# A decoder layer on one core: order of the experts' gate and up products, start of the expert sums, and spread of LN2's vectors changed

## The chip, the cores and the metric

One Trainium2 chip, of which the kernel uses one core: TensorE (PE), VectorE (DVE), ScalarE (ACT), GpSimd (POOL), SyncE (SP, which here only issues DMAs) and 16 DMA engines. The metric is device time of one execution in microseconds, lower is better: the median of several runs. One execution is profiled apart.

## The reference

One layer on 512 tokens of width 1024. A token mixer (dilated attention, sliding-window attention with sinks, gates, output projection) is followed by LN1, then a mixture of 32 experts of which each token takes 4, then LN2:

```
x   = layer_norm(alpha * x + mix, ln1_g, ln1_b)          # alpha = 2 ** 0.25, eps = 1e-5
top_val, top_idx = top_k(x @ router_w + router_b, 4); gates = softmax(top_val)
gt  = min(xb @ w_gate[e] + b_gate[e], 7);  up = clip(xb @ w_up[e] + b_up[e], -7, 7)
ys  = (gt * sigmoid(1.702 * gt) * (up + 1)) @ w_down[e] + b_down[e]
ffn = sum over a token's 4 experts of gate * ys
out = layer_norm(alpha * x + ffn, ln2_g, ln2_b)
```

All weights are float32, and all 32 experts' weights (32 x 12 MB) are read.

## The kernel before

**Up to the experts.** The mixer is a long sequence of TensorE matmuls over chunks of `w_in`, `w_proj` and `w_out`. At its start `first_chunk` loads x and the first `w_in` chunk in quarters on SP's queue, while POOL's queue writes zeros from the tile `warm` into `acc_dram`, the DRAM tensor of the expert sums, in 16 pieces. `norm_tile(t)` does LN1 for one of four token tiles; the result y stays in `r_tiles[t]` and is written to `y_dram` by POOL's queue (for t = 0 also to 128 spare rows). The router follows: `route_places` finds each token's place with its experts, `slots` turns places into row indices and gathers an expert's rows of y with an indirect DMA on POOL's queue, `rank_experts` orders the experts by their number of tokens, `route_weights` makes the softmax weights.

**The experts.** Experts run in an order by rank (`TURNS`). The 18 with most tokens have two blocks of rows: block A of 64 rows (its products are 128 x 512 in PSUM) and block B of 32 rows (128 x 256). The other 14 have block A alone; experts 0 and 1 of the order have two blocks, 2 and 3 one, the last three one. `ffn` does one expert: its 12 weight chunks (4 gate, 4 up, 4 down, each 1.05 MB and two rows of K) go through `load_expert` to a ring of 21 slots in several pools, of which the slots of `ring_d` lie where `r_tiles` were. `load_expert` is called in the order of use, and the loads stand on SP's queue in that order, each behind the last reader of its slot; eight DMAs of SP are under way at most. `gate_up(n)` does bias, gate and up products of block n (0 is A, 1 is B); `glu(n)` the clamps, gelu and product on VectorE and ACT; then `transposed` (TensorE, copied by ACT) and `down`. Gate and up of block A have a PSUM bank each (tags `a0`, `a1`), those of B share one (tag `b`). `add_rows` adds the weighted rows to `acc_dram` with an indirect DMA on POOL's queue. `midway` computes the index lists of the expert after the next.

Each engine's instructions run in the order in which the program's scheduler puts them, which is that of the text unless an instruction isn't ready by its estimate; `tc.issue_after(ins)` keeps what it encloses behind `ins` on the same engine.

**The end.** The rows of the last expert are not added in DRAM: `goes` is a 0/1 matrix with which TensorE spreads `ys_last` over the tokens into `psf`. Before that, `free_tiles(6)` takes six ring slots: LN2's two vectors come in as broadcasts to 128 partitions, y as four loads (`y_last`), the sums as four loads (`r_last`), and `load_sums` makes alpha * y + sum on VectorE. A loop under `tc.If` handles experts with more rows than their blocks hold; with these inputs its body doesn't run, but all engines pass its test (line 981; line 980 loads the number into registers). `last_rows(t)` does `psf`, the sum with its mean, and the variance; `last_norm(t)` normalizes on ACT, multiplies by g on VectorE, adds b on POOL or VectorE, and stores 512 KB.

Of the kernel before, what the change touches and what calls it, by code (L numbers as in the profile page):

```python
# [8 lines left out]
F32 = mybir.dt.float32  # L9
# [48 lines left out]
def decoder_kernel(tc, d):  # L58
# [19 lines left out]
    def load_chunk(src, n, name, pool=None):  # L78
        t = (pool or ring_a).tile([P, 2048], F32, name=name, tag="w")
        nc.sync.dma_start(t[:, :n], src[:, :n])  # L80
        return t

    n_loaded = [0]

# [8 lines left out]
    def load_expert(src, name):  # L93

        ring = next_ring()
        if ring is not None:
            t = load_chunk(src, 2048, name, ring)
            return [t[:, :1024], t[:, 1024:]]
        t = [spl.tile([P, 1024], F32, name=f"{name}{n}", tag=f"w{n}") for n in "hl"]
        for n in range(2):  # L100
            nc.sync.dma_start(t[n], src[:, n * 1024:(n + 1) * 1024])
        return t
# [32 lines left out]
    for n in range(8):  # L135
        mm(ps, warm[:, :P], warm, True, True)

    dpool = tc.alloc_tile_pool(name="dp", bufs=1, space=DRAM)
    y_dram = dpool.tile([S + P, D], F32, name="y_dram")
    acc_dram = dpool.tile([S + P, D], F32, name="acc_dram")  # L140
# [377 lines left out]
    ring_c = tc.alloc_tile_pool(name="ring_c", bufs=RING[3], side="right")  # L518
    rings.append(ring_c)
    mo1 = tc.alloc_tile_pool(name="mo1", bufs=1, side="right")  # L520
    p_y = tc.alloc_tile_pool(name="p_y", bufs=1, side="right")
# [28 lines left out]

    last = {}

    def norm_stats(r, sums, sq, pool, name):
# [5 lines left out]
        A.activation(rs, rs, AF.Sqrt, bias=C[:, C_COL + 4:C_COL + 5], scale=1.0 / D)  # L559
        V.reciprocal(rs, rs)  # L560
        return nmu, rs
# [16 lines left out]
    def norm_tile(t):  # L578
# [4 lines left out]
        with tc.high_priority():  # L583
            for n in range(2):
                cs = slice(n * 512, (n + 1) * 512)
                V.scalar_tensor_tensor(y[:, cs], y[:, cs], ALPHA, mix[t][n], op0=ALU.mult, op1=ALU.add,
                                       accum_out=sums[:, n:n + 1])
            sq = yT[0].rearrange("p k c -> p (k c)").bitcast(BF16)
            nmu, rs = norm_stats(y, sums, sq, p_ln, f"a{t}")
        for n in range(2):  # L590
# [218 lines left out]
    def ffn(e, chunk, state, sw, xt, midway=None, next_rows=None):  # L809
# [10 lines left out]

        def gate_up(n):
            slots_n, pieces, tiles = (64, 2, 4) if n == 0 else (32, 4, 2)
            for g in range(2):
                packed_mm(n, pg[n][g], sel[:, :slots_n], bh[:, g * D:(g + 1) * D], n == 0 or g == 0, False)
            for g in range(2):
                for k in range(KT):
                    packed_mm(n, pg[n][g], xt[n][:, k % tiles, k // tiles, :], chunks[4 * g + k // 2][k % 2],
                              False, k == KT - 1)

        def glu(n):  # L830
            gt, up = pg[n]
            w = 512 if n == 0 else 256
            h = mo.tile([P, w], F32, name=f"up{n}{e}", tag=f"up{n}")
            V.tensor_scalar(gt, gt, 7.0, None, op0=ALU.min)  # L834
            A.activation(gt, gt, AF.Gelu_apprx_sigmoid)  # L835
            V.tensor_scalar(h, up, 7.0, -7.0, op0=ALU.min, op1=ALU.max)  # L836
            V.scalar_tensor_tensor(h, h, 1.0, gt, op0=ALU.add, op1=ALU.mult)
            return h
# [44 lines left out]
    def rank_experts():  # L883
# [12 lines left out]
        V.tensor_copy(order_i, order[0:1])  # L896

    rank_experts()
    for tp in range(2):
# [3 lines left out]
    rings.append(tc.alloc_tile_pool(name="ring_d", bufs=RING[4], side="right", reuse_waits="tile"))  # L903

    def expert(i):
        def midway():
            if i == 0:
                for e in range(FIXED):
                    sws[e] = late_weights(e, states[e], first_info[e], psX, "t")
            if i + 2 < NE:  # L910
                r = TURNS[i + 2]
# [24 lines left out]
    ys_last, = expert(NE - 1)  # L936
    free = free_tiles(6)
    goes = free[0][:, :S]
# [7 lines left out]
    ln2 = free[1].rearrange("p (n c) -> p n c", n=2)  # L946
    nc.sync.dma_start(ln2[:, 0, :], d["ln2_g"].partition_broadcast(P))
    nc.sync.dma_start(ln2[:, 1, :], d["ln2_b"].partition_broadcast(P))
    tiles = [t.rearrange("p (n c) -> p n c", n=2) for t in free[2:]]
    y_last = [tiles[t // 2][:, t % 2, :] for t in range(NT)]  # L950
    r_last = [tiles[2 + t // 2][:, t % 2, :] for t in range(NT)]
# [56 lines left out]


    def last_rows(t):  # L1010

        r = r_last[t]
        part_sums = mo.tile([P, 2], F32, name=f"fsums{t}", tag="fsums", bufs=NT)
        for n in range(2):
            cs = slice(n * 512, (n + 1) * 512)
            ps = psG.tile([P, S], F32, name=f"psf{t}{n}", tag=f"a{n}")
            half = slice(64 * n, 64 * n + 64)
            ts = slice(t * P, (t + 1) * P)
            mm(ps, goes[half, ts], ys_last[half, :], True, True, (64 * n, 0))
            V.scalar_tensor_tensor(r[:, cs], ps, 1.0, r[:, cs], op0=ALU.mult, op1=ALU.add,  # L1020
                                   accum_out=part_sums[:, n:n + 1])
        sq = mo.tile([P, 512], F32, name=f"fsq{t}", tag="up0").bitcast(BF16)
        nmu, rs = norm_stats(r, part_sums, sq, mo, f"f{t}")
        V.tensor_tensor(nmu, nmu, rs, op=ALU.mult)  # L1024
        return nmu, rs
# [23 lines left out]
def _consts():  # L1049
# [8 lines left out]
    c[:, C_COL + 3] = i % 32  # L1058
    c[:, C_COL + 4] = EPS
    for n, m in enumerate((64, 32)):  # L1060
        pieces = P // m
# [73 lines left out]
```

## Time and profile before

| | us |
|---|---|
| median of 3 runs | 1568.25 |
| lowest, highest | 1567.65, 1575.2 |
| the profiled execution | 1572.44 |
| its span, first to last instruction | 1570.6 |

Of the span TensorE is busy 94%, VectorE 30%, ACT 21%, POOL 10%; the mean granted TensorE clock is 0.973 of full speed. DMA moves 477.38 MB. A span of a matmul is modelled, so a busy TensorE is not TensorE at its peak. Times in all rows are microseconds from the span's start.

### The profile page before, as it was taken

How to read it: one execution, taken by the hardware profiler on the slowest of the kernel's cores; microseconds unless marked ns; L12 is line 12 of the kernel's file. 1: busy time of each engine (PE TensorE's matmuls, PEld its weight loads, DVE VectorE, ACT ScalarE, POOL GpSimd, SP SyncE). 2: the span in 40 equal slices, each digit the busy share in tenths (PEclk: the TensorE clock that was granted, in tenths of full speed). 3: DMA queues.
4: the chain of work that ended last, by engine and by line, in shares of the span. 5: the costliest groups of instructions: out<-in, count | busy, mean ns of one | idle time of the engine just before them, and what ended most of it. 6: DMA issues, size and time to landing. Idle time of an engine off the chain costs nothing. (4 is left out here: it accounts for less than half of the span.)

```text
span 1570.6 us, 24882 instructions
## 1 busy us (share of the span) xinstructions
PE 1469.7 (94%) x10022; PEld 808.3 (51%) x10022; DVE 467.0 (30%) x1348; ACT 322.3 (21%) x697; POOL 161.7 (10%) x133
## 2 busy tenths in 40 slices
PE   8999999999996999999999899989999899889872
PEld 6987777788885444535344353325335253323220
DVE  3133667764337412111211121111211112111105
ACT  4233556633323101100101011000100001000003
POOL 2000000000001011111201111111211111111002
PEclk9989999999997999999999999999999999999995
DMA  8111110332387599999999999999999999999992
GB/s 311 59 50 54 54 44 18 137 133 90 131 344 299 220 362 410 408 404 409 405 405 408 408 408 407 405 409 407 409 411 400 412 400 407 412 393 412 410 404 89
DMA packets 85527, 477.38 MB, mean 304 GB/s; under 512 B 10528, under 2 KB 13088, under 8 KB 39968
## 3 DMA queue, kind: packets, MB, share of 16 engines
q1 hardware_dynamic: 73440, 449.78, 70.7%
q0 software_dynamic: 11968, 25.96, 6.3%
q8 instruction: 81, 1.33, 0.3%
q14 instruction: 38, 0.31, 0.1%
HBM read 458.40 MB, written 17.30 MB: 303 GB/s over the span
## 5 line engine op out<-in xcount | busy, mean ns | idle before, releaser
L834 DVE TENSOR_SCALAR pga<-pga 128x512 f32<-128x512 f32 x32 | 22.4, 699 | 385.1 <-PE pga L806 374.4
L798 POOL DMA_INDIRECT acc_dram<-ys,ix x49 | 78.1, 1594 | 365.7 <-issue 131.9
L734 POOL DMA_INDIRECT xg<-y_dram,ix x50 | 61.0, 1220 | 501.4 <-issue 358.6
L836 DVE TENSOR_SCALAR up<-pga 128x512 f32<-128x512 f32 x32 | 22.1, 691 | 230.7 <-PE pga L806 230.7
L790 ACT COPY th<-pth 128x512 f32<-128x512 f32 (+1 forms) x50 | 25.3, 506 | 293.8 <-PE pm L64 257.6
L117 DVE TENSOR_TENSOR wlin<-win,whin 128x1024 fp32r<-128x1024 f32 x42 | 51.2, 1224 | 115.3 <-ACT whin L116 109.9
L849 ACT ACTIVATE ys<-pda,sw 128x512 f32<-128x512 f32 x32 | 22.0, 688 | 229.2 <-PE pda L806 229.2
L835 ACT ACTIVATE pga<-pga 128x512 f32<-128x512 f32 x32 | 18.6, 582 | 245.5 <-DVE pga L834 245.5
L116 ACT CAST whin<-win 128x1024 fp32r<-128x1024 f32 x42 | 44.1, 1050 | 65.8 <-PE psk L64 15.3
L64 PE MATMUL psg<-xh,wlin 128*128 128x512 f32 x128 | 50.1, 392 | 0.0
L64 PE MATMUL psg<-xh,whin 128*128 128x512 f32 x128 | 50.1, 391 | 0.0
L64 PE MATMUL psg<-xl,whin 128*128 128x512 f32 x128 | 49.9, 390 | 0.0
L790 ACT COPY tx<-ptx 128x512 f32<-128x512 f32 (+1 forms) x50 | 24.4, 516 | 100.6 <-PE ptx L788 100.6
L806 PE MATMUL pga<-we_l,tx 128*64 128x512 f32 x152 | 42.3, 597 | 2.5 <-DMA we_l<-in_w_exp_dram 2.5
L806 PE MATMUL pga<-we_h,tx 128*64 128x512 f32 x152 | 42.4, 597 | 1.7 <-DMA we_h<-in_w_exp_dram 1.7
L540 POOL MEMSET obf<- 128x128 bf16 x1 | 0.2, 205 | 412.5 <-DVE merged L512 412.5
L834 DVE TENSOR_SCALAR pgb<-pgb 128x256 f32<-128x256 f32 x18 | 7.8, 432 | 104.2 <-PE pgb L806 104.2
L64 PE MATMUL mx<-whwo,merged 128*128 128x512 f32 x128 | 38.1, 400 | 0.0
L739 DVE TENSOR_SCALAR sel<-C,order 96x64 bf16<-96x64 f32 x30 | 7.4, 247 | 92.3 <-PE pdb L806 92.3
L64 PE MATMUL psv<-wlin,xh 128*128 128x256 f32 x96 | 34.4, 358 | 0.0
L64 PE MATMUL psv<-whin,xl 128*128 128x256 f32 x96 | 34.4, 358 | 0.0
L64 PE MATMUL psv<-whin,xh 128*128 128x256 f32 x96 | 34.4, 358 | 0.0
(1310 smaller groups left out, 3018.4 us busy)
## 6 DMA issues: line engine op xcount, KB each, us to landing
we_h<-in_w_exp_dram SPq DMA_DIRECT2D x54, 512.0 KB
we_l<-in_w_exp_dram SPq DMA_DIRECT2D x54, 512.0 KB
win<-in_w_in_dram SPq DMA_DIRECT2D x21, 1024.0 KB
wpj<-in_w_proj_dram SPq DMA_DIRECT2D x8, 640.0 KB
wo<-in_w_out_dram SPq DMA_DIRECT2D x4, 1024.0 KB
y_dram<-r POOLq DMA_DIRECT2D x5, 512.0 KB, 3.4
x<-in_xT_dram SPq DMA_DIRECT2D x4, 512.0 KB
acc_dram<-warm POOLq DMA_DIRECT2D x16, 128.0 KB, 6.3
```

What stands on the lines that cost most here:

```text
L64: T.matmul(out, lhsT, rhs, start=start, stop=stop)
L116: A.copy(wh[:, :n], src)
L117: V.tensor_tensor(wl[:, :n], src, wh[:, :n], op=ALU.subtract)
L734: G.indirect_dma_start(out=x, out_offset=None, in_=table, in_offset=bass.IndirectOffsetOnAxis(ap=ix[:, 0:1], axis=0))
L739: V.tensor_scalar(sel, C[:96, C_COL + 3:C_COL + 4].to_broadcast([96, 64]), which, None, op0=ALU.is_equal)
L790: A.copy(t, pt.rearrange("p (b h s) -> p b h s", b=tiles, h=pieces))
L798: G.indirect_dma_start(out=acc, out_offset=bass.IndirectOffsetOnAxis(ap=state[0][n][1][:, 0:1], axis=0), in_=ys[n], in_offset=None, comput ...
L806: last["mm"] = T.matmul(out[m * h:m * h + m, :], lhsT, rhs[:, h * w:(h + 1) * w], start=start, stop=stop, tile_position=(0, m * h), skip_g ...
L834: V.tensor_scalar(gt, gt, 7.0, None, op0=ALU.min)
L835: A.activation(gt, gt, AF.Gelu_apprx_sigmoid)
L836: V.tensor_scalar(h, up, 7.0, -7.0, op0=ALU.min, op1=ALU.max)
L849: A.mul(y, pd[n], sw()[n])
```

## The change

1. The zero writes to `acc_dram` go. After LN1 of a token tile, POOL's queue writes y to `acc_dram` too: tiles 0 to 2 behind their write to `y_dram`, tile 3 ahead of `rank_experts`. The tail no longer loads y and no longer adds alpha * y. To make up for alpha, the softmax denominators are multiplied by alpha, and LN2's epsilon is divided by alpha squared.
2. `gate_up` and `glu` are split. The order of an expert's products becomes: biases A, gate A, biases B, gate B, up A, up B; clamp and gelu of gate A stand behind gate A, those of gate B behind up B.
3. `ln2_rows`, in `midway` of the last expert: LN2's vectors are loaded as rows of one partition, spread by four matmuls with a row of ones, and copied from PSUM by ACT.
4. The tail: the sums' loads stand behind the last weight load on SP's queue; `psf` uses eight PSUM banks in place of two; two tiles are under way at a time in place of three; all adds of b on VectorE; the last tile is normalized on VectorE with two fused operations per half; each tile is stored in two halves.

```diff
-    for t in range(NT):
-        for n in range(4):
-            G.dma_start(acc_dram[t * P:(t + 1) * P, n * 256:(n + 1) * 256], warm.bitcast(F32))
...
         G.dma_start(y_dram[t * P:(t + 1) * P, :], y)
         if t == 0:
             G.dma_start(y_dram[S:, :], y)
+        if t < NT - 1:
+            G.dma_start(acc_dram[t * P:(t + 1) * P, :], y)
...
+        V.tensor_scalar(se, se, ALPHA, None, op0=ALU.mult)
         V.reciprocal(se, se)
...
-        gate_up(0)
-        hA = glu(0)
+        biases(0)
+        products(0, 0)
+        gate_of(0)
         if n_blocks > 1:
             with tc.issue_after(last["mm"].ins):
-                gate_up(1)
-            hB = glu(1)
+                biases(1)
+                products(1, 0)
+        with tc.issue_after(last["mm"].ins):
+            products(0, 1)
+        hA = gated(0)
+        if n_blocks > 1:
+            with tc.issue_after(last["mm"].ins):
+                products(1, 1)
+            gate_of(1)
+            hB = gated(1)
...
+    G.dma_start(acc_dram[(NT - 1) * P:S, :], r_tiles[NT - 1])
     rank_experts()
...
+    def ln2_rows():
+
+        row, out = free_tiles(2)
+        ones = mo.tile([1, P], F32, name="ones")
+        G.memset(ones, 1.0)
+        nc.sync.dma_start(row[:1, :D], d["ln2_g"][None, :])
+        nc.sync.dma_start(row[:1, D:], d["ln2_b"][None, :])
+        for n in range(4):
+            cs = slice(n * 512, (n + 1) * 512)
+            ps = (psG, psD)[n % 2].tile([P, S], F32, name=f"psl{n}", tag="b")
+            mm(ps, ones, row[:1, cs], True, True)
+            A.copy(out[:, cs], ps)
+        ln2.extend((out[:, :D], out[:, D:]))
...
-    free = free_tiles(6)
+    free = free_tiles(3)
...
-    nc.sync.dma_start(ln2[:, 0, :], d["ln2_g"].partition_broadcast(P))
-    nc.sync.dma_start(ln2[:, 1, :], d["ln2_b"].partition_broadcast(P))
...
-    for t in range(NT):
-        nc.sync.dma_start(y_last[t], y_dram[t * P:(t + 1) * P, :])
...
             nc.sync.dma_start(r_last[t], acc_dram[t * P:(t + 1) * P, :])
-            V.scalar_tensor_tensor(r_last[t], y_last[t], ALPHA, r_last[t], op0=ALU.mult, op1=ALU.add)
-
-    load_sums()
+
+    with tc.issue_after(last["load"].ins):
+        load_sums()
...
+    banks = [(psG, "a0"), (psG, "a1"), (psG, "b"), (psD, "b"), (psX, "t"), (psX, "t"), (psX, "t"), (psD, "a")]
...
     def last_norm(t, nmu, rs):
         r = r_last[t]
-        A.activation(r, r, AF.Identity, bias=nmu, scale=rs)
+        g, b = ln2
+        if t < NT - 1:
+            V.tensor_tensor(nmu, nmu, rs, op=ALU.mult)
+            A.activation(r, r, AF.Identity, bias=nmu, scale=rs)
         for n in range(2):
             cs = slice(n * 512, (n + 1) * 512)
-            V.tensor_tensor(r[:, cs], r[:, cs], ln2[:, 0, cs], op=ALU.mult)
-            (V if n and t > 1 else G).tensor_tensor(r[:, cs], r[:, cs], ln2[:, 1, cs], op=ALU.add)
-        nc.sync.dma_start(d["out"][t * P:(t + 1) * P, :], r)
+            if t < NT - 1:
+                V.tensor_tensor(r[:, cs], r[:, cs], g[:, cs], op=ALU.mult)
+                V.tensor_tensor(r[:, cs], r[:, cs], b[:, cs], op=ALU.add)
+            else:
+                V.scalar_tensor_tensor(r[:, cs], r[:, cs], nmu, g[:, cs], op0=ALU.add, op1=ALU.mult)
+                V.scalar_tensor_tensor(r[:, cs], r[:, cs], rs, b[:, cs], op0=ALU.mult, op1=ALU.add)
+            nc.sync.dma_start(d["out"][t * P:(t + 1) * P, cs], r[:, cs])
...
-    stats = [last_rows(t) for t in range(3)]
+    stats = [last_rows(t) for t in range(2)]
     for t in range(NT):
+        if t + 2 < NT:
+            stats.append(last_rows(t + 2))
         last_norm(t, *stats[t])
-        if t + 3 < NT:
-            stats.append(last_rows(t + 3))
```

`biases(n)` and `products(n, g)` hold the loops of `gate_up` for one block and one of gate (g = 0) and up (g = 1); `gate_of(n)` clamps and activates the gate, `gated(n)` clamps up and multiplies.

## Rows read from the trace of the kernel before

**Rows 1.** Busy time by stage: stretch, length, engines (instructions), clock, DMA share, GB/s.
```profile
17.00:485.00 468.00, 467.40 (x2427) 381.24 (x2427) 230.71 (x503) 193.45 (x455) 2.97 (x5) 0.98 0.31 113
485.00:511.00 26.00, 13.90 (x90) 11.32 (x88) 18.92 (x57) 7.52 (x15) 5.53 (x6) 0.59 0.94 351
...
800.00:1500.00 700.00, 657.74 (x5158) 271.68 (x5150) 117.23 (x446) 68.69 (x138) 94.08 (x67) 1.00 1.02 407
```
**Rows 2.** The same view in steps of 5 us, where the weight stream starts.
```profile
515.00:520.00 5.00, 5.00 (x26) 1.55 (x24) 0.71 (x4) 0.00 (x0) 0.00 (x0) 1.00 0.00 0
...
560.00:565.00 5.00, 5.00 (x74) 2.22 (x74) 1.38 (x2) 0.00 (x0) 0.00 (x0) 1.00 0.56 145
```
**Rows 3.** Timeline of SP's queue, 440 to 620: start, length, DMA issued.
```profile
527.46 0.34 SPq L80 DMA_DIRECT2D we__4536<-in_w_exp_dram  x1
...
545.60 0.33 SPq L80 DMA_DIRECT2D we__4634<-in_w_exp_dram  x1
...
563.28 0.33 SPq L80 DMA_DIRECT2D we__4750<-in_w_exp_dram  x1
...
571.45 0.33 SPq L101 DMA_DIRECT2D we_l<-in_w_exp_dram  x1
...
580.08 0.33 SPq L80 DMA_DIRECT2D we__4803<-in_w_exp_dram  x1
...
591.90 0.33 SPq L80 DMA_DIRECT2D we__4948<-in_w_exp_dram  x1
```
**Rows 4.** Waits of SP's queue, 565 to 600: total us, times, longest.
```profile
SPq L101 <- DMA we__4752<-in_w_exp_dram: 1.9, 1, 1.9
SPq L80 <- DMA we__4803<-in_w_exp_dram: 1.7, 1, 1.7
```
**Rows 5.** Timeline of PE, expert 0: its first block's fifth chunk and the second block's bias.
```profile
519.16 1.88 PE L806 MATMUL pga<-we__4061,tx 128*64 128x512 f32 x8
...
526.12 0.40 PE L806 MATMUL pgb<-bh,sel 96*32 96x256 bf16 x8
```
**Rows 6.** Timeline of the tail, all engines, 1500 to 1571.
```profile
1522.73 5.43 SPq L957 DMA_DIRECT2D free<-acc_dram  x4
...
1527.02 1.89 PE L806 MATMUL pda<-we__11344,th 128*64 128x512 f32 x8
...
1538.19 2.45 DVE L958 SCALAR_TENSOR_TENSOR free<-free,free 128x1024 f32<-128x1024 f32 x2 [0.73 <-SPq L981]
...
1540.85 2.08 PE L66 MATMUL psf<-ys,free 64*128 64x512 f32 x4 [11.94 <-DVEq L981]
```
**Rows 7.** Lines 980 and 981: ns min/median/max, first and last start.
```profile
L980 PEldq TENSOR_LOAD <-total x1: 486/486/486, 1525.2 to 1525.2; - x1
...
L981 SPq EVENT_SEMAPHORE  x9: 17/17/17, 1529.3 to 1539.5; - x9
...
L981 PEldq COMPARE_BRANCH  x1: 6157/6157/6157, 1525.8 to 1525.8; - x1
```
**Rows 8.** Timeline of the tail, VectorE in LN2.
```profile
1542.93 0.69 DVE L1020 SCALAR_TENSOR_TENSOR free<-psf,free 128x512 f32<-128x512 f32 x1 [2.28 <-PE psf L66]
...
1552.26 0.68 DVE L1032 TENSOR_TENSOR free<-free,free 128x512 f32<-128x512 f32 x1
...
1556.17 4.63 DVE L1032 TENSOR_TENSOR free<-free,free 128x512 f32<-128x512 f32 x4
...
1565.17 1.63 DVE L1033 TENSOR_TENSOR free<-free,free 128x512 f32<-128x512 f32 x1
```
**Rows 9.** Timeline of PE at the start, with idle time and what ended it.
```profile
16.91 0.50 PE L64 MATMUL psq<-xh,whin 128*128 128x512 f32 x1 [0.64 <-ACT xh L186]
```
**Rows 10.** Waits of SP's queue, 440 to 515.
```profile
SPq L80 <- DMA y_dram<-r: 10.1, 2, 7.8
```
**Rows 11.** Timeline of POOL, 440 to 600.
```profile
491.79 0.53 POOL L596 DMA_DIRECT2D y_dram<-r  x1 [3.23 <-DVE r L595]
...
503.66 1.03 POOL L734 DMA_INDIRECT xg<-y_dram,ix  x1 [11.34 <-DVE ix L731]
```

More of the change, by code (lines that the diff above doesn't have):

```diff
@@ L79, in load_chunk @@
         t = (pool or ring_a).tile([P, 2048], F32, name=name, tag="w")
-        nc.sync.dma_start(t[:, :n], src[:, :n])
+        last["load"] = nc.sync.dma_start(t[:, :n], src[:, :n])
         return t
+    last = {}
     n_loaded = [0]
@@ L100, in load_expert @@
         for n in range(2):
-            nc.sync.dma_start(t[n], src[:, n * 1024:(n + 1) * 1024])
+            last["load"] = nc.sync.dma_start(t[n], src[:, n * 1024:(n + 1) * 1024])
         return t
@@ L136, in decoder_kernel @@
         mm(ps, warm[:, :P], warm, True, True)
-    dpool = tc.alloc_tile_pool(name="dp", bufs=1, space=DRAM)
-    y_dram = dpool.tile([S + P, D], F32, name="y_dram")
-    acc_dram = dpool.tile([S + P, D], F32, name="acc_dram")
-    for t in range(NT):
-        for n in range(4):
-            G.dma_start(acc_dram[t * P:(t + 1) * P, n * 256:(n + 1) * 256], warm.bitcast(F32))
     oT_h = [p_out.tile([P, S], F32R, name=f"oTh{c}") for c in range(10)]
@@ L519, in decoder_kernel @@
     rings.append(ring_c)
+    dpool = tc.alloc_tile_pool(name="dp", bufs=1, space=DRAM)
+    y_dram = dpool.tile([S + P, D], F32, name="y_dram")
+    acc_dram = dpool.tile([S + P, D], F32, name="acc_dram")
     mo1 = tc.alloc_tile_pool(name="mo1", bufs=1, side="right")
@@ L549, in decoder_kernel, with norm_stats @@
     G.memset(known[:, :, 1], 1.0)
-    last = {}
-    def norm_stats(r, sums, sq, pool, name):
+    def norm_stats(r, sums, sq, eps, pool, name):
         nmu = pool.tile([P, 1], F32, name="nmu" + name, tag="nmu", bufs=2)
@@ L558, in norm_stats @@
         A.activation(sq, r, AF.Square, bias=nmu, accum_out=rs)
-        A.activation(rs, rs, AF.Sqrt, bias=C[:, C_COL + 4:C_COL + 5], scale=1.0 / D)
+        A.activation(rs, rs, AF.Sqrt, bias=eps, scale=1.0 / D)
         V.reciprocal(rs, rs)
@@ L588, in norm_tile @@
             sq = yT[0].rearrange("p k c -> p (k c)").bitcast(BF16)
-            nmu, rs = norm_stats(y, sums, sq, p_ln, f"a{t}")
+            nmu, rs = norm_stats(y, sums, sq, C[:, C_COL + 4:C_COL + 5], p_ln, f"a{t}")
         for n in range(2):
@@ L819, in ffn, with biases, products, gate_of @@
             pd.append(psD.tile([P, S], F32, name=f"pdb{e}", tag="b")[:, :256])
-        def gate_up(n):
-            slots_n, pieces, tiles = (64, 2, 4) if n == 0 else (32, 4, 2)
+        def biases(n):
             for g in range(2):
[L824 to L833, printed above, removed]
+                packed_mm(n, pg[n][g], sel[:, :64 if n == 0 else 32], bh[:, g * D:(g + 1) * D], n == 0 or g == 0, False)
+        def products(n, g):
+            tiles = 4 if n == 0 else 2
+            for k in range(KT):
+                packed_mm(n, pg[n][g], xt[n][:, k % tiles, k // tiles, :], chunks[4 * g + k // 2][k % 2],
+                          False, k == KT - 1)
+        def gate_of(n):
+            gt = pg[n][0]
             V.tensor_scalar(gt, gt, 7.0, None, op0=ALU.min)
             A.activation(gt, gt, AF.Gelu_apprx_sigmoid)
+        def gated(n):
+            gt, up = pg[n]
+            h = mo.tile([P, 512 if n == 0 else 256], F32, name=f"up{n}{e}", tag=f"up{n}")
             V.tensor_scalar(h, up, 7.0, -7.0, op0=ALU.min, op1=ALU.max)
@@ L909, in midway @@
                     sws[e] = late_weights(e, states[e], first_info[e], psX, "t")
+            if i == NE - 1:
+                ln2_rows()
             if i + 2 < NE:
@@ L945, in decoder_kernel @@
         V.tensor_scalar(goes[:, t * P:(t + 1) * P], C[:, C_IOTA:C_IOTA + P], to_t[:, t:t + 1], None, op0=ALU.is_equal)
-    ln2 = free[1].rearrange("p (n c) -> p n c", n=2)
-    nc.sync.dma_start(ln2[:, 0, :], d["ln2_g"].partition_broadcast(P))
-    nc.sync.dma_start(ln2[:, 1, :], d["ln2_b"].partition_broadcast(P))
-    tiles = [t.rearrange("p (n c) -> p n c", n=2) for t in free[2:]]
-    y_last = [tiles[t // 2][:, t % 2, :] for t in range(NT)]
-    r_last = [tiles[2 + t // 2][:, t % 2, :] for t in range(NT)]
-    for t in range(NT):
-        nc.sync.dma_start(y_last[t], y_dram[t * P:(t + 1) * P, :])
+    r_last = [free[1 + t // 2][:, t % 2 * D:(t % 2 + 1) * D] for t in range(NT)]
     def load_sums():
@@ L1015, in last_rows @@
             cs = slice(n * 512, (n + 1) * 512)
-            ps = psG.tile([P, S], F32, name=f"psf{t}{n}", tag=f"a{n}")
+            pool, tag = banks[2 * t + n]
+            ps = pool.tile([P, S], F32, name=f"psf{t}{n}", tag=tag)
             half = slice(64 * n, 64 * n + 64)
-            ts = slice(t * P, (t + 1) * P)
-            mm(ps, goes[half, ts], ys_last[half, :], True, True, (64 * n, 0))
+            mm(ps, goes[half, t * P:(t + 1) * P], ys_last[half, :], True, True, (64 * n, 0))
             V.scalar_tensor_tensor(r[:, cs], ps, 1.0, r[:, cs], op0=ALU.mult, op1=ALU.add,
@@ L1021, in last_rows @@
                                    accum_out=part_sums[:, n:n + 1])
[L1022 to L1025, printed above, removed]
+        sq = mo.tile([P, 512], F32, name=f"fsq{t}", tag=("up0", "t0h")[t % 2]).bitcast(BF16)
+        return norm_stats(r, part_sums, sq, C[:, C_COL + 5:C_COL + 6], mo, f"f{t}")
     def last_norm(t, nmu, rs):
         r = r_last[t]
-        A.activation(r, r, AF.Identity, bias=nmu, scale=rs)
+        g, b = ln2
@@ L1059, in _consts @@
     c[:, C_COL + 4] = EPS
+    c[:, C_COL + 5] = EPS / ALPHA ** 2
     for n, m in enumerate((64, 32)):
```

1 line of the change is left out of this document (added).

## Prediction

> **What bounds the kernel now.** I read the busy windows first, by stage. Up to 485 us TensorE works without a gap at nearly full clock while DMA is mostly idle; from 800 to 1500 us, in the middle of the 32 experts, DMA is at a share of 1.02 and 407 GB/s [rows 1]. So the body is bound by the stream of expert weights: 384 loads of 1.05 MB. TensorE counts as busy there too (657.74 of 700 us), but the DMA has no idle time to give. A faster expert in the body therefore buys nothing; what counts is when the stream becomes continuous and what follows its end.
>
> Then the same view in 5 us steps: between the first weights and 566 us the stream stands still twice, wholly at 515 us and partly at 560 us [rows 2]. The SP timeline says why: one load is issued at 527.46, then others at 545.60, 563.28 and 580.08 [rows 3], each just after TensorE's last use of the slot. 21 slots are full and TensorE empties them. From 591.90 SP instead waits for the landing of the load eight before it ([rows 4] name that load), so DMA sets the pace from there on.
>
> Last the tail. The last weight lands at about 1525.2: there TensorE's queue gets past it to the register load for the `If` [rows 7], and the last product ends at 1528.9 [rows 6]. But the first `psf` matmul starts only at 1540.85, after VectorE's fourth ALPHA·y sum, which began its last pair at 1538.19 on loads issued from 1522.73 [rows 6]. From there to the span's end, 1570.6, are 29.75 us of LayerNorm with TensorE nearly idle.
>
> **The change, part by part.**
>
> *Gate products first (two-block experts only).* Today block A runs gates and ups (eight chunks), then B runs both. A gate chunk is free only when B has used it. The four up chunks of A take from 519.16 plus one chunk's step: bias of B starts at 526.12 [rows 5], so about 6.9 us (1.72 each). The change puts B's four gate chunks ahead of A's ups, so four slots come free 6.9 us earlier: 527.46 becomes 520.6 and 563.28 becomes 556.4. Up slots and down slots come free when they did, since TensorE's total is the same. So not all 6.9 passes on; I follow the loads. A load issued onto a nearly idle DMA lands 5.6 us later: the one behind 563.28 landed at 571.45, when SP's wait for it ended [rows 3, 4], less one load of 2.5 us is 568.9. The load issued at 580.08 landed at 591.90 by the same reading [rows 3, 4], 23.0 us for eight loads, 2.9 each with gathers and scatters. In the changed kernel expert 0's four downs, issued from 545.60, land from 551.2 to 559.9, the next four from 562.8, the ups of expert 1 (free at about 566.6) by 583, and the load of 580.08, which does not move, cannot land before 580.08 + 5.6 = 585.7. Against 591.9 that is 6.2 us earlier, and from there the stream is continuous (SP is eight loads, some 20 us, ahead), so its end moves by the same: 6.2 us. Bounds: 0 if each earlier release only opens another gap later, 8.7 if downs move too. In one-block experts gate clamp and gelu ran beside the ups already; nothing changes there.
>
> *Zero writes at the start become writes of y.* Sixteen writes of 128 KB (2.1 MB, some 5 us of DMA) leave the time in which x arrives. At 16.91 TensorE loses 0.64 us to the cast of x's last part [rows 9], which waits for its load. TensorE sets the pace from there to 485, so what it gains passes on. I take 1.0, bounds 0 and 2. The 2.1 MB come back as four POOL writes around the routing. The gathers for expert 0 wait for their indices until 503.66, while y's last write, issued at 491.79 [rows 11], had landed some 7.8 us later, SP's longest wait for such a write [rows 10]: by 499.6. 0.5 to 1 MB more costs DMA 1.3 to 2.6 us in a queue with 4 us of room: I take 0, bounds -1.5 (weights behind the last write leave the gathers alone) and +1.5.
>
> *Sums begin as y; LN2's vectors by TensorE.* Four loads of y (2.1 MB), two broadcasts (1.05 MB) and four VectorE sums of 1.22 us leave the tail. After the last weight only the four loads of sums are queued: 2.1 MB at 407 GB/s is 5.2 us. Today 5.2 MB take 12.8 us, to 1538.0, and SP's last wait event at the `If` is at 1539.5 [rows 7], 1.5 later. So SP is through 6.7 us after the last weight. TensorE's queue needs 0.5 us for the register load and 6.16 us for its branch [rows 7], which today hides behind the loads and now lies level with them: 6.7 to 6.9. I take 6.9, against 15.65 now (1525.2 to 1540.85): 8.7 us less; bounds 5 and 9. The page "DMA: Bandwidth & Descriptors", section "Where 436 GB/s comes from", of the Trainium skill has about 358 GB/s as HBM's limit for one core; the stage row measures 407 [rows 1], so the measurement decides; by the page the sums would take 5.9 us and the tail 0.7 more.
>
> The vectors now cost four one-row matmuls and four ACT copies between the last expert's ups and its transposes. VectorE's clamp and product there take 1.5 us anyway; at 0.43 us per matmul (two passes of a chunk's eight in 1.72) and copies of 0.7 the transposes come 1 to 2 us later. The downs then end about 4 us after the last weight, as now, and the branch covers it: 0. Without that cover it costs 2.
>
> *LN2 itself.* Today `psf` uses two banks, so its matmuls wait for VectorE; now eight banks. VectorE's work: eight sums of 0.69 (in pairs 1.31) [rows 8], 5.3 us; small ones 0.9; for three tiles twelve products and sums at 0.64 (the 0.60 to 0.68 of a lone L1032 [rows 8]), 7.7; the last tile four fused at 0.66, 2.6. That is 16.5, plus 2.1 until the first `psf` pair is out and about 2 of waits for TensorE and ACT: 20.5, against 25.95 now (1540.85 to 1565.17 + 1.63 [rows 6, 8]). The end after VectorE, 3.8 us now, I put at 3.6 with half-size stores. Together 24.1 instead of 29.75: 5.6 less; bounds 2 (each tile again waits 1.3 us for ACT) and 8 (no waits). All adds now on VectorE would be a loss if its pace beside POOL were its own: four L1032 took 4.63 us, 1.16 each [rows 8]; twelve at that price are 6.2 us more, and LN2 gains nothing. "SBUF — State Buffer", section "Who interferes with whom", of the Trainium skill says that a VectorE instruction with two SBUF inputs and a GpSimd one that reads SBUF hold a shared port in turn; the lone 0.60 agrees, and the 0.64 stands.
>
> *The rest.* ALPHA in the weights is two tiny VectorE operations, epsilon a constant: 0.
>
> Sum: 1.0 + 6.2 + 8.7 + 5.6 = 21.5 us. The profiled execution took 1572.44 (span 1570.6 and 1.8 around it), 4.2 above the median of 1568.25; off its own time that gives 1550.9, off the median 1546.8, which I forecast as 1547.
>
> **The rivals.**
>
> *The stream does not move.* Gaps just go elsewhere, since downs at 545.60 and 580.08 stay put. For: only four of twelve slots per expert come earlier. Against: 580.08 issued into a backlog of 11.8 us to landing, where 5.6 would do. It gives 1547 + 6.2 = 1553.
>
> *The tail finds another wait.* The LN2 vectors' rows land behind the last ups, or TensorE's branch starts later, or VectorE keeps waiting for ACT; 4 to 8 us: about 1553. For: TensorE does its queue in order, so a late row holds up the downs. Against: the rows are asked for ahead of the downs.
>
> *The change does little.* Both of these together, with LN2 at its lower bound: 1568.25 - 1 - 5 - 2 = 1560.
>
> *Routing is held up.* "SBUF — State Buffer", section "SBUF: two separate sides", of the Trainium skill warns that a POOL-issued DMA cannot be described while VectorE holds the shared port. As a mechanism here: four more POOL writes in a stretch where VectorE is busy 18.92 of 26 us [rows 1] push y's last write past 503.66, then gathers and expert 0 start later, at most by the 7.8 us that SP waited for that write [rows 10]: 1555 at worst. POOL's present 0.53 us for a write there [rows 11] speaks against.
>
> *Slower: TensorE becomes the bound.* The new order is pinned, so bubbles that other matmuls filled could stay open in each of 18 two-block experts. TensorE's idle time from 800 to 1500 is 42 us [rows 1]; beyond 42 / 18 = 2.4 us per expert each microsecond counts. To end 0.5% slower it must lose 42 + 21.5 + 7.8, that is 4 us per expert; at 4.5 the time is 1547 + 39 = 1586. Against: same products, and the clamps still have 3.5 us of B's ups to run beside.
>
> **How the numbers follow.** Forecast 0.60, no stream gain 0.12, tail wait 0.13, routing 0.04, little change 0.06, slower 0.05. A measurement of this kernel tells 0.5% (7.8 us) from no change, so faster ends at 1560.4. Part of "little" lies beyond it: faster 0.87, same 0.08, slower 0.05. With all bounds at their best ends the gain is 2 + 1.5 + 8.7 + 9 + 8 = 29.2 (1539), with all at their worst 5.5 (1563). The range, 1539 to 1560, takes in the rivals up to 1560 and leaves out the slower case and about half of "little".
>
> **What would show it.** Right: SP's issues of 527.46 and 563.28 some 7 us earlier and those of 545.60 and 580.08 hardly; the last weight about 7 us earlier; `psf` some 7 us behind it; no L958; LN2 from `psf` to the end near 24 us. Wrong: a gap in the stream after 590, TensorE waiting for LN2's rows, or POOL's gathers after 505.

## The result, and the profile after

The changed kernel takes 1552.65 us (median of 4 runs, 1551.35 to 1553.49) against 1570.31 (1567.65 to 1575.2) for the kernel before: a ratio of 0.9883, with a 95% interval of 0.9854 to 0.9912, 17.7 us. In a second comparison (experiment 13) it took 1551.58 against 1571.87, a ratio of 0.9871 (0.9856 to 0.9886). The profiled execution took 1551.86, its span 1550.1, 20.5 less than the span of before. 1547 had been forecast, in a range of 1539 to 1560.

I divide each span at four marks: the first gather's issue on POOL, the first gate product of expert 0, the first product of the last expert's last up chunk, and `psf`. In us:

| profiled execution | first gather | to gate product | to last up chunk | to `psf` | to the end | span |
|---|---|---|---|---|---|---|
| before | 503.66 | 7.36 | 1004.19 | 25.64 | 29.75 | 1570.6 |
| after | 501.52 | 8.54 | 1000.87 | 16.84 | 22.33 | 1550.1 |
| difference | -2.14 | +1.18 | -3.32 | -8.80 | -7.42 | -20.5 |

**The stream's start.** Busy time by stage of the changed kernel, as [rows 1]:
```profile
17.00:485.00 468.00, 466.23 (x2429) 380.93 (x2428) 230.63 (x509) 192.93 (x456) 3.29 (x7) 0.99 0.32 112
485.00:511.00 26.00, 14.85 (x88) 11.67 (x89) 19.03 (x60) 7.76 (x16) 7.04 (x9) 0.52 0.94 369
800.00:1500.00 700.00, 661.53 (x5150) 255.56 (x5146) 119.65 (x452) 68.65 (x138) 94.72 (x67) 1.00 1.02 406
```
The body is what it was: DMA at a share of 1.02. The gain is at both ends. The same view in 5 us steps, as [rows 2]:
```profile
515.00:520.00 5.00, 5.00 (x50) 1.93 (x50) 1.31 (x8) 0.58 (x1) 0.00 (x0) 1.00 0.00 0
520.00:525.00 5.00, 5.00 (x62) 2.01 (x52) 2.87 (x22) 0.00 (x1) 0.00 (x0) 1.00 0.79 269
...
540.00:545.00 5.00, 5.00 (x45) 2.28 (x44) 3.17 (x16) 1.72 (x4) 1.77 (x2) 1.00 0.61 241
545.00:550.00 5.00, 5.00 (x62) 2.20 (x56) 0.00 (x0) 0.47 (x1) 0.47 (x1) 1.00 0.78 199
...
560.00:565.00 5.00, 5.00 (x26) 1.58 (x22) 0.00 (x0) 0.00 (x0) 0.00 (x0) 1.00 1.00 417
```
The timeline of SP's queue in the changed kernel, the issues that answer to [rows 3]:
```profile
519.90 0.33 SPq L80 DMA_DIRECT2D we__4526<-in_w_exp_dram  x1
...
545.23 0.33 SPq L80 DMA_DIRECT2D we__4624<-in_w_exp_dram  x1
...
556.02 0.33 SPq L80 DMA_DIRECT2D we__4740<-in_w_exp_dram  x1
...
579.97 0.33 SPq L80 DMA_DIRECT2D we__4793<-in_w_exp_dram  x1
```
527.46 has become 519.90 and 563.28 has become 556.02; 545.60 and 580.08 stand, as the forecast said. The dead time at 560 us is gone and that around 520 us is shorter, but a new gap stands at 540 to 550 us, where DMA's share was 1.00 and 1.02 before: the load of 545.23 still waits for TensorE, 11.2 us long.

**Routing.** Timeline of POOL, PE and SP around the first gathers, as [rows 11]:
```profile
490.25 0.53 POOL L910 DMA_DIRECT2D acc_dram<-r  x1
...
501.52 1.03 POOL L734 DMA_INDIRECT xg<-y_dram,ix  x1 [2.90 <-DVE oh L722]
502.71 0.33 SPq L80 DMA_DIRECT2D we__4524<-in_w_exp_dram  x1
...
508.11 1.11 PE L788 MATMUL ptx<-C,xg 128*128 128x128 f32 x4 [5.15 <-DMA xg<-y_dram,ix]
```
And the waits of SP's queue there, as [rows 10]:
```profile
SPq L80 <- DMA y_dram<-r: 7.9, 1, 7.9
...
SPq L80 <- DMA acc_dram<-r: 6.1, 1, 6.1
```
SP now waits for the second write of y as well, since this load overwrites y's rows. So it issues the load at 502.71, among the gathers; before, at 499.70, four us ahead of them.

**The tail.** Timeline of SP, PE and VectorE, as [rows 6, 8], the ACT product `ys` among them:
```profile
1508.49 3.70 SPq L981 DMA_DIRECT2D free<-acc_dram  x4
...
1512.80 3.78 PE L64 MATMUL psl<-free,ones 1*128 1x512 f32 x8
...
1516.51 1.06 PE L788 MATMUL pth<-C,up 128*128 128x128 f32 x4
...
1524.34 1.88 PE L806 MATMUL pda<-we__11352,th 128*64 128x512 f32 x8
...
1526.28 0.69 ACT L852 ACTIVATE ys<-pda,sw 128x512 f32<-128x512 f32 x1 [8.04 <-PE pda L806]
...
1527.77 3.70 PE L66 MATMUL psf<-ys,free 64*128 64x512 f32 x16 [1.54 <-PEq L1005]
...
1528.90 0.69 DVE L1046 SCALAR_TENSOR_TENSOR free<-psf,free 128x512 f32<-128x512 f32 x1 [14.49 <-PE psf L66]
...
1545.47 1.40 DVE L1064 SCALAR_TENSOR_TENSOR free<-free,rsf,free 128x512 f32<-128x512 f32 x2
```
The `If` of the changed kernel (line 1005), ns and start, as [rows 7]:
```profile
L1005 SPq EVENT_SEMAPHORE  x9: 17/17/17, 1512.7 to 1527.9; - x9
...
L1005 PEldq COMPARE_BRANCH  x1: 5077/5077/5077, 1522.4 to 1522.4; - x1
L1005 ACTq COMPARE_BRANCH  x1: 50/50/50, 1526.8 to 1526.8; - x1
```
No VectorE sum stands ahead of `psf` any more. In this execution it waits for TensorE's branch, which ends at 1527.5; SP's last event is level with it. In seven of the executions below (3 to 7, 10, 13) the branch is shorter, and `psf` waits for ACT instead (experiment 13). All 16 `psf` matmuls run through without a stop, and LN2 is VectorE's work with 1.6 us of waits in all.

### The profile page after: what moved, and what is told of

Its sections match the earlier page's. It is cut to its first block, busy times and chain, and to the rows that moved or that the text cites. A ratio compares the mean times of both kernels' runs of the same rounds, so it can differ in the third digit from the quotient of the medians.

```text
span 1550.1 us, 24873 instructions
## 1 busy us (share of the span) xinstructions
PE 1468.9 (95%) x10030; PEld 787.7 (51%) x10030; DVE 460.5 (30%) x1351; ACT 322.8 (21%) x700; POOL 145.9 (9%) x116
## 5 line engine op out<-in xcount | busy, mean ns | idle before, releaser
L833 DVE TENSOR_SCALAR pga<-pga 128x512 f32<-128x512 f32 x32 | 22.4, 699 | 398.0 <-PE pga L806 398.0
L788 PEld LDWEIGHTS pth<-C,up 128*128 128x128 f32 x164 | 17.3, 142 | 30.1 <-issue 22.4
```

Of the source, the lines that this page charges most:

```text
L788: T.transpose(pt[:, b * P:(b + 1) * P], src[:, b * P:(b + 1) * P], ident)
```

## The experiments

The table has the same marks for each; its first column shifts by itself from execution to execution (below), so the verdicts are read from the others. Experiments 3 to 8, 10 and 11 are one execution each; 1, 2, 12 and 13 have medians. There is no experiment 9.

| execution | first gather | to gate product | to last up chunk | to `psf` | to the end | span |
|---|---|---|---|---|---|---|
| 1 order alone | 502.90 | 7.35 | 1000.76 | 24.95 | 29.7 | 1565.7 |
| 2 order undone | 500.55 | 8.63 | 1005.93 | 16.46 | 22.3 | 1553.9 |
| 3 zero writes kept | 503.09 | 8.75 | 1001.47 | 17.73 | 22.4 | 1553.4 |
| 4 late y writes | 496.90 | 6.04 | 1001.41 | 16.08 | 22.4 | 1542.8 |
| 5 rows aside | 499.47 | 8.82 | 1001.67 | 17.65 | 22.3 | 1549.9 |
| 6 adds on POOL | 499.27 | 8.81 | 1000.87 | 16.06 | 23.2 | 1548.2 |
| 7 two banks | 501.52 | 8.87 | 1000.97 | 17.73 | 23.2 | 1552.3 |
| 8 y loads kept | 499.74 | 8.93 | 1000.88 | 19.50 | 23.7 | 1552.7 |
| 10 load late | 503.17 | 6.37 | 1000.53 | 17.73 | 22.3 | 1550.1 |
| 11 rows in stream | 503.60 | 8.56 | 1000.94 | 15.09 | 22.3 | 1550.5 |
| 12 both moves | 499.56 | 5.65 | 1000.39 | 15.53 | 22.3 | 1543.4 |
| 13 changed again | 500.58 | 8.88 | 1001.89 | 16.24 | 22.3 | 1549.9 |

**1 and 2: the order of the products, alone and undone.** The kernel before with the split functions and the new order; the changed kernel with `gate_up` and `glu` and the old order. In short form, without the `issue_after` lines:
```diff
-        gate_up(0); hA = glu(0); gate_up(1); hB = glu(1)
+        biases(0); products(0, 0); gate_of(0); biases(1); products(1, 0)
+        products(0, 1); hA = gated(0); products(1, 1); gate_of(1); hB = gated(1)
```


> The kernel before with one thing changed: gate products of both blocks ahead of the up products. Theory (the weight stream is released earlier, and nothing else of the experts counts): the SP issues of 527.46 and 563.28 come about 7 us earlier, those of 545.60 and 580.08 stay within 0.5 us, the later loads and the last weights come 5 to 6 us earlier (on the changed kernel they came 4.7 earlier with the start of the kernel changed too), the tail keeps its length, and the time falls by 5 to 6 us, ratio 0.9965. Rival (the gaps only go elsewhere): the last weights within 1 us of before, ratio 1.000.

> The changed kernel with the old order of products, and clamps and gelu behind them as before; everything else stays changed. Theory: the stream loses its advance, the last weights land 4 to 5 us later than in the changed kernel (within 1 us of the kernel before), the rest of the tail stays as short as in the changed kernel, span 1554 to 1556. Rival (the start of the kernel, not the order, moved the stream): the last weights stay 4.7 us earlier than before, span 1550 to 1551.

Alone: 1567.88 against 1572.23, a ratio of 0.9978 (0.996 to 0.9996). Undone: 1556.43, 0.99 (0.9868 to 0.9932) of before, where the full change has 0.9883. SP's issues move as forecast both times (556.10 with the new order, 562.58 with the old). The last up chunk comes 3.4 us sooner behind the first gate product (before to 1) and 4.0 to 5.1 (2 to 13 and to after). What became of the forecast's 6.2 is told by SP's timeline, the kernel before first, then experiment 1:
```profile
644.38 0.33 SPq L80 DMA_DIRECT2D we__5367<-in_w_exp_dram  x1
...
1505.35 0.33 SPq L80 DMA_DIRECT2D we__11344<-in_w_exp_dram  x1
```
```profile
639.80 0.33 SPq L80 DMA_DIRECT2D we__5367<-in_w_exp_dram  x1
...
1501.14 0.33 SPq L80 DMA_DIRECT2D we__11344<-in_w_exp_dram  x1
```
The same load goes out 7.3 us sooner at 559 us, not sooner at 580 us, 4.6 us sooner at 640 us and 4.2 at the last; over the 361 loads from 640 us on the median is 4.6 (2.9 to 6.7). So the gain is settled by 640 us, smaller than forecast already there, and then passes on to the end. The time fell by 4.4 us, a little under the 5 to 6 expected.

**3: zero writes kept**, into a spare DRAM tensor, all else as changed.
```diff
+    for t in range(NT):
+        for n in range(4):
+            G.dma_start(spare[t * P:(t + 1) * P, n * 256:(n + 1) * 256], warm.bitcast(F32))
```


> The changed kernel with the sixteen zero writes of 128 KB at the start put back, into a spare DRAM tensor that nobody reads. Theory (the 2 us gained at the start are spent between 485 and 510 us, where loads of weights, the writes of y and the gathers share the DMA engines, so they pay for the added writes of y): TensorE reaches the routing 2 us later than in the changed kernel, the gathers land 1.5 to 2 us later, first gate product at 511.5 to 512, the load after expert 1's first down product about 581.5, span 1551.5 to 1552. Rival (the gathers land when they land, whatever the start does): routing 2 us later, but first gate product at 510 and span 1550.

The first gate product came at 511.84, 1.8 later than after, as the theory has it, and the later marks with it, though the span of 1553.4 lies above both expectations. By itself this decides little, since the first gather moves by more among executions with the same mixer. Over all executions the mixer's first V product (`psv`) starts at 42.84 us on average with zero writes (43.24, 42.73, 42.55) and at 41.43 without (eleven executions, 40.30 to 42.96): 1.4 us, with overlap at the edge.

**4: late y writes.** The y writes of tiles 2 and 3 stand behind the gathers, and so does the load that overwrites them.
```diff
-        if t < NT - 1:
+        if t < 2:
             G.dma_start(acc_dram[t * P:(t + 1) * P, :], y)
...
+    with tc.issue_after(last_gather.ins):
+        for t in (2, 3):
+            G.dma_start(acc_dram[t * P:(t + 1) * P, :], r_tiles[t])
```


> The changed kernel with the writes of y into the expert sums for tiles 2 and 3 put behind the four gathers of experts 0 and 1 on POOL's queue; the weight load whose slot lies where tiles 2 and 3 were then is issued behind them as well. Theory (the gathers wait for a DMA backlog to which these writes and that load belong): the gathers' rows are in TensorE 1.5 to 3 us earlier, at 506.5 to 508 instead of 509.4, and everything that TensorE paces up to 580 us moves along, span 1547.5 to 1548.5. Rival (the gathers' own time, not the backlog): rows at 509 to 509.5 and span 1550.

The span fell by 7.3 us, far more than expected. The timeline of experiment 4, POOL and PE:
```profile
496.90 1.03 POOL L734 DMA_INDIRECT xg<-y_dram,ix  x1 [2.90 <-DVE oh L722]
...
501.15 1.54 PE L789 MATMUL ptx<-C,xg 128*128 128x128 f32 x6 [2.82 <-DMA xg<-y_dram,ix]
...
502.54 1.17 POOL L913 DMA_DIRECT2D acc_dram<-r  x2
```
From gather to gate product 2.5 us are saved (8.54 to 6.04), inside what was expected. But the first gather itself is 4.6 us earlier, and the edit is not what moved it. Busy time of two stretches in the mixer, the changed kernel first, then experiment 4; the third number from the right is the granted clock:
```profile
100.00:120.00 20.00, 20.00 (x79) 15.34 (x78) 11.88 (x26) 10.42 (x48) 0.00 (x0) 0.83 0.11 45
...
160.00:180.00 20.00, 20.00 (x82) 15.32 (x81) 11.26 (x35) 11.28 (x49) 0.00 (x0) 0.83 0.00 0
```
```profile
100.00:120.00 20.00, 20.00 (x90) 15.85 (x90) 13.62 (x38) 11.85 (x53) 0.00 (x0) 1.00 0.10 41
...
160.00:180.00 20.00, 20.00 (x100) 15.32 (x97) 14.42 (x51) 11.51 (x46) 0.00 (x0) 1.00 0.00 1
```
In this one execution the granted clock was 1.00 (2.4 GHz) in both stretches; in the thirteen others its mean from 100 to 120 us was 0.57 to 0.91. The first V product starts at 42.34 and 41.93 in the two, and the first write of y, ahead of all that the edit moves, at 471.83 and 467.20: 4.6 us apart, of which 4.2 arise between these marks. Only the 2.5 belong to the edit.

**10: load late.** Which of the two moved things held the gathers? All y writes as in the changed kernel; the loads into the two slots under y wait for a small POOL write behind the gathers.
```diff
...
+    with tc.issue_after(last_gather.ins):
+        for n in range(RING[4]):
+            G.memset(rings[4].tile([P, 2048], F32, name=f"hold{n}", tag="w")[:1, :1], 0.0)
```


> All four y writes stay ahead of the gathers as in the changed kernel; only the first weight load into the slots under the y rows (and so every load behind it on SP) waits until the gathers are issued. Judged by the time from the first gather's issue to the first gate product, which was 7.36 and 7.35 us with before's writes, 8.5 to 8.9 us in six executions with the y writes ahead, and 6.04 us with two y writes and this load both behind the gathers. Theory, the weight load competes with the gathers for DMA: 6.0 to 6.6 us. Rival, the two y writes delay them by themselves: 8.5 to 8.9 us. A value near 7.3 would share it.

```profile
503.17 1.05 POOL L734 DMA_INDIRECT xg<-y_dram,ix  x1 [3.07 <-DVE ix L731]
...
507.75 1.54 PE L789 MATMUL ptx<-C,xg 128*128 128x128 f32 x6 [3.32 <-DMA xg<-y_dram,ix]
...
508.56 0.33 SPq L80 DMA_DIRECT2D we__4361<-in_w_exp_dram  x1
```
That is the timeline of experiment 10. 6.37 us from gather to product: the theory. With the y writes where they were and the loads out of the way, the gathers are quick; the writes' own share is at most the 0.3 to 0.7 us to experiments 4 and 12. The edit holds back both loads into these slots, one more than experiment 4 does.

**5: rows aside.** LN2's four one-row products into four banks instead of two, copied by VectorE.
```diff
-            ps = (psG, psD)[n % 2].tile(..., tag="b");  A.copy(out[:, cs], ps)
+            pool, tag = ((psG, "b"), (psD, "b"), (psX, "t"), (psX, "t"))[n]
+            ps = pool.tile(..., tag=tag);  V.tensor_copy(out[:, cs], ps)
```


> The changed kernel with LN2's vectors spread into four PSUM banks instead of two and copied out by VectorE instead of ACT, so that the four matmuls wait for no copy and the copy of the transposes on ACT has nothing ahead of it. In the changed kernel the last expert's transposes begin 3.7 us after its last up product against 1.5 before. Theory (this delay of 2.2 us reaches the end, since TensorE's branch begins when its last products are queued): transposes 1.5 to 2.0 us after the last up product, first matmul of LN2 1.5 to 2 us earlier against the last up product (15.0 instead of 16.8 us behind the last up chunk's first product), span about 1548. Rival (the branch or the loads of the sums hide it): first matmul of LN2 still 16.8 us behind, span 1550.

My theory fell: it is not the copies that hold the eight matmuls. PE's group in experiment 5 (busy us, mean ns):
```profile
L64 PE MATMUL psl<-free,ones 1*128 1x512 f32 x8 | 4.4, 695 | 0.0
```
Without waits they take 4.4 us at a granted clock of 0.83, against 3.78 with the copies at 1.00 in the changed kernel, and 3.70 without any copy at 1.00 in experiment 11: the matmuls themselves take this time. `psf` is no earlier.

**11: rows in stream.** The same matmuls in the next to last expert, where TensorE waits for weights anyway; ACT's copies stay in the last.
```diff
+            if i == NE - 2:
+                ln2_rows()        # row loads, four one-row products into four banks
             if i == NE - 1:
-                ln2_rows()
+                ln2_copies()      # four ACT copies into the ring tile
```


> The eight one-row matmuls of LN2's vectors move to the next to last expert, into PSUM banks that are free there; only the ACT copies out of them stay in the last expert. Theory, after the change TensorE's own queue ends the tail, so its 3.7 us between the last up product and the transposes are on the path: the transposes follow some 1.5 us behind the last up products and psf starts 14 to 15 us behind the last up chunk's first product (16.1 to 17.7 in six executions with the matmuls in between). Rival, the landing of the last down weights sets the tail: the down products then wait for DMA and psf stays at 16 to 17.7 us. The span falls by 2 us or by nothing, apart from the start's drift of some us.

PE's timeline in experiment 11:
```profile
1483.71 3.70 PE L64 MATMUL psl<-free,ones 1*128 1x512 f32 x8
...
1516.62 0.66 PE L788 MATMUL pth<-C,up 128*128 128x128 f32 x4 [1.37 <-DVE up L840]
...
1528.19 3.70 PE L66 MATMUL psf<-ys,free 64*128 64x512 f32 x16 [1.41 <-PEq L1014]
```
`psf` comes 15.09 us behind the last up chunk, 1 to 2.6 less than in the executions with the matmuls in between (without experiment 8): mostly the theory, just outside its 14 to 15. The transposes come 2.1 us sooner behind that chunk than in the changed kernel, but the first two down chunks give 0.85 back: TensorE's granted clock was 0.67 there, after waits of 1.37 and 0.73 us, against 0.80. `psf` again waits for the branch (4.17 us here).

**6: adds on POOL**, and **7: two banks**, LN2's two changes undone one by one.
```diff
-                V.tensor_tensor(r[:, cs], r[:, cs], b[:, cs], op=ALU.add)
+                (V if n and t > 1 else G).tensor_tensor(r[:, cs], r[:, cs], b[:, cs], op=ALU.add)
```
```diff
-            pool, tag = banks[2 * t + n]
+            pool, tag = psG, f"a{n}"
```


> The changed kernel with LN2's adds of b back on POOL for tiles 0 and 1 and for half of tile 2, as before. Theory (VectorE's operations with two SBUF inputs and POOL's take turns): multiplications beside POOL take 1.1 to 1.2 us each instead of 0.64, and LN2 from its first matmul to the end takes 24 to 26 us instead of 22.3. Rival (VectorE is relieved of five operations of 0.64 and runs at its own pace): 20 to 22 us.

> The changed kernel with LN2's first products in two PSUM banks as before instead of eight. Theory (VectorE is what LN2 is bound by, and the banks only shorten its first waits): 1 to 2.5 us longer from the first matmul to the end than the 22.3 us of the changed kernel. Rival (the banks made the difference, with TensorE's clock falling between the separate matmuls): 4 us or more. Second rival: no difference.

Both make LN2 23.2 us instead of 22.3. That is between the two expectations for experiment 6 and just under the theory's 1 to 2.5 us for experiment 7. In experiment 6 VectorE's products stretch as in [rows 8]; its timeline, VectorE and POOL:
```profile
1535.73 4.62 DVE L1060 TENSOR_TENSOR free<-free,free 128x512 f32<-128x512 f32 x4
...
1536.56 4.92 POOL L1061 TENSOR_TENSOR free<-free,free 128x512 f32<-128x512 f32 x3 [1.06 <-DVE free L1060]
```
A product takes 1.16 beside POOL's adds, and 0.68 alone. The Trainium skill ("SBUF — State Buffer", "Who interferes with whom") has the two engines hold one port in turn, and the trace agrees. Only four of the six products run beside POOL's adds. In experiment 7 the second pair of `psf` waits 0.79 us for VectorE's sums and VectorE then 0.28 to 0.54 us for each next pair; PE's timeline:
```profile
1531.00 1.73 PE L66 MATMUL psf<-ys,free 64*128 64x512 f32 x4 [0.79 <-DVE free L1046]
```

**8: y loads kept.** Four loads of y ahead of the sums' loads, into tiles that nobody reads.
```diff
-    free = free_tiles(3)
+    free = free_tiles(5)
...
+        for t in range(NT):
+            nc.sync.dma_start(free[3 + t // 2][:, t % 2 * D:(t % 2 + 1) * D], y_dram[t * P:(t + 1) * P, :])
```


> The changed kernel with the four loads of y (2.1 MB) put back ahead of the loads of the sums, into tiles that nobody reads, without the sums on VectorE. Theory (after the last weight the loads of the sums are ready before TensorE is through its branch, with 0 to 2 us to spare, and nobody passes the test of the loop before they have landed): 5.2 us more of loads delay the first matmul of LN2 by 3 to 5 us. Rival: the first matmul stays where it is (16.8 us behind the last up chunk's first product) and only VectorE's first sum waits for the loads.

PE's timeline and line 1007, the `If`, in experiment 8:
```profile
1529.05 5.13 PE L66 MATMUL psf<-ys,free 64*128 64x512 f32 x16 [2.57 <-PEq L1007]
```
```profile
L1007 PEldq COMPARE_BRANCH  x1: 6097/6097/6097, 1522.6 to 1522.6; - x1
```
`psf` came 19.50 us behind the last up chunk, 2.7 more than after: between the two. The loads do hold up SP, whose last event at the `If` stands 20.2 us behind the last up chunk, against 17.0 after and 15.4 to 15.6 in the ten other executions of this tail. But `psf` was released by the branch, and it started at 1529.05, ahead of SP's last event at 1529.8. This branch took 6.10 us instead of 5.08, and from the first down product to the third chunk's were 5.8 us instead of 4.3, at a granted clock of 0.60 instead of 0.80: 2.4 of the 2.7. The slow down chunks need no y loads, since experiment 7 has them too (5.8 us, 0.59) with `psf` at 17.73; the 1.8 us between these two are the branch. Whether the loads made it long is not settled (see the last section), nor what they cost.

**12 and 13: both moves, and the changed kernel beside them.** Experiment 4's and 11's edits together.

> The changed kernel with the two y writes and the load that follows them behind the gathers, and the one-row matmuls in the next to last expert. Theory: both savings hold and add, 2.2 to 2.8 us from the first gather to the first gate product (6.0 to 6.4 us instead of 8.5 to 8.9) and 1 to 2 us between the last up chunk and psf (14.3 to 15.5 us instead of 16.1 to 17.7), so 3.5 to 4.5 us less than the changed kernel at the median of the same chip, about 1548.5 by the medians so far. Rival: what the start gains is given back in the queue-paced stream, as part of the gate order's gain was, and only 1 to 2 us are left.

> The changed kernel, unaltered, to have its median beside the one with both moves on one chip and to see how far executions of one program lie apart before the routing. Both theories: 1551 to 1553.5 us. If the stretch of lower clock between 100 and 180 us differs from execution to execution, the first gather's issue (501.52 us in the first profile) moves by some us with it, while first gather to first gate product (8.54 us) and last up chunk to psf (16.84 us) stay within 0.5 and 1 us.

`psf` and the branch in experiment 13, PE's timeline and line 1005:
```profile
1527.59 3.70 PE L66 MATMUL psf<-ys,free 64*128 64x512 f32 x16 [0.79 <-ACTq L1005]
```
```profile
L1005 PEldq COMPARE_BRANCH  x1: 3957/3957/3957, 1523.0 to 1523.0; - x1
```
The same program, but its branch took 3.96 us in place of 5.08 and ended with the last down product; `psf` then waited for ACT, which makes `ys` and passes the `If` behind it. In all seven executions of this kind `psf` starts 2.7 us behind the first product of the last down chunk, against 3.4 in the first profile of the changed kernel.

Both moves: 1545.39 us (1543.66 to 1549.19), 0.9838 of before (0.9822 to 0.9853). The changed kernel on the same chip: 1551.58 (1549.86 to 1553.22). That is 6.2 us at the median, and the runs don't overlap; 3.5 to 4.5 had been expected. Of the profiled 6.5 us, 3.2 lie between gather and gate product (more than the 2.2 to 2.8 expected), 1.5 in the stream, 0.7 ahead of `psf` (less than the 1 to 2 expected), and 1.0 is the first gather's own drift. The places that the edits touch thus account for 3.9; the 1.5 in the stream is not explained. The start's gain passes on to the end of the stream, against the rival.

## Why the prediction was right, and where not

**What bounds the kernel: right.** DMA's share in the body stayed at 1.02, and what changed is the stream's start and what follows its end.

**Gate products first: right mechanism, size off.** The issues of 527.46 and 563.28 moved as forecast, and the step "from there the stream is continuous, so its end moves by the same" held: 4.6 us at 640 us, 4.6 at the median of all later loads (experiment 1). Mis-sized is the term itself, "23.0 us for eight loads ... against 591.9 that is 6.2 us earlier": 4.6, and 3.4 to 5.1 between the marks. The new gap at 540 to 550 us shows that "gaps just go elsewhere" is true of a part; why 1.6 us are missing was not tried.

**The start: the step that failed is the y writes at 0.** The gain of 1.0 was there (1.4 in the mean). But the price of the y writes, 0 with a bound of +1.5, was 1.2 to 1.6 us (8.5 to 8.9 us from gather to product, 7.36 before), so nothing is left of it. I had looked at the writes in the queue. What counts is who waits for them: SP's next load, which overwrites y, now goes out amid the gathers. That is experiment 10. The rival "routing is held up" is not what happened: the gathers were issued no later than before, they took longer.

**The loads after the last weight: 8.7 forecast, 8.8 measured, in part by luck.** Sums and broadcasts went off the path, and SP's end lies level with the branch's, as forecast. But in the changed kernel the last weight no longer sets this stretch. TensorE's register load for the `If` starts 10.0 us behind the last up chunk in the kernel before and in 1, 11 and 12, and 10.9 to 12.5 us with the one-row matmuls in the last expert: its own queue sets it. Those matmuls take 3.7 us where I had 1 to 2 (0.93 each at a granted clock of 1.00, not 0.43). In the profile the branch was 1.1 us shorter than its 6.16 and the register load 0.9 later, so the two errors cancelled; over the executions of this tail without the y loads `psf` came 15.1 to 17.7 us behind the last up chunk. "The branch covers it: 0" was wrong; moving the matmuls saves 0.5 to 2.6 us (11, 12). So the rival "tail finds another wait" was there too, with a smaller price. What the y loads, the broadcasts and VectorE's sums were each worth was not measured; the trace of before shows only that `psf` waited for the sums [rows 6].

**LN2: 5.6 forecast, 7.4 measured.** Three small terms of the sum: the first `psf` pair was out after 1.1 us, not 2.1 (TensorE's granted clock was 1.00 there, 0.50 before); VectorE's stretch from 1528.90 to 1546.87 is 18.0, not 18.5; the end after it 3.2, not 3.6. The 0.64 for an operation (measured 0.60 to 0.68) was right. POOL's adds and the two banks are worth 0.9 us each (6, 7).

**Slower: no.** TensorE's idle time from 800 to 1500 went from 42 to 38.5 us, 0.2 us per two-block expert, far from the 4 that it takes. TensorE never waited for LN2's rows, and the gathers did not slip past 505 us.

**Sum.** Forecast 1.0 + 6.2 + 8.7 + 5.6 = 21.5; the spans differ by 20.5, of which 1 or so is drift of the mixer. The nearness is partly luck: the stream fell 2.9 short and the y writes cost 1.2, while LN2 gave 1.8 and the time ahead of the first gather 1.1 more than forecast. Off the median of the three first runs this came out 5.7 us low; before's median was 1570.3 to 1572.2 in the later comparisons, 2 to 4 us above the one that the forecast took off from.

## What to carry to other kernels

When a buffer gets one more reader, price not only that reader but the load that overwrites the buffer: its issue moves, and what it then collides with may cost more than the transfer. When the transfers at the end of a stream are cut, look at which queue ends next, and move what stands in it back into the stretch where that engine waits anyway. And measure between marks inside the span: a 2.5 us effect was legible from gather to product, where the whole times of the same program spread over 3.6 us.

## What the runs showed of the hardware

**The clock in the mixer differs between executions.** From 100 to 120 us the granted clock was 0.57 to 1.00, from 160 to 180 us 0.83 to 1.00, with the same matmuls. The first gather's issue lay between 496.90 and 503.60 us in the eleven executions with the changed kernel's mixer. From the first V product to that issue took 455.0 us in experiment 4, at 1.00 in both stretches, and 462.5 in experiment 10, at 0.57 and 0.83.

**TensorE's branch over the `If` is long and varies.** It took 3.60 to 6.22 us in the fourteen executions; ACT's took 0.05 and VectorE's 0.08. The three long ones (6.16 before, 6.22 in experiment 1, 6.10 in 8) are those with loads of y behind the last weight, and DMA's share during them was 0.97, 0.98 and 0.55; in the eleven others, 3.60 to 5.08 us, it was 0.07 to 0.42. In the seven short ones (3.60 to 3.96) the branch ended within 0.25 us of the end of the last down product. The length goes roughly with DMA's traffic; whether the traffic causes it was not tried.

**Gathers suffer from one 1.05 MB load beside them:** from 5.7 to 6.4 us between first gather and first gate product (4, 10, 12) to 8.5 to 8.9 (after and the eight others with the load at 0.9 to 1.6 us behind the first gather).
